# Seven quarter-block products for the gate columns as well, in 14 of 31 pairs, with small changes to the attention values and the first network

## The chip, the core and the metric

The kernel runs on one core of one Trainium2 chip. The metric is the device time of one execution in microseconds (us), as the median of several runs. All numbers below are of that core.

The core's engines work side by side, each through its own list of instructions in order: TensorE (matrix products; PE in the profile, PEld for the loading of its weights), VectorE (DVE), ScalarE (ACT), GpSimd (POOL) and SyncE (SP), which here issues the transfers from memory. Products land in PSUM, where this kernel has eight tiles of 128 x 512 numbers; everything else is in SBUF.

## What is computed

An encoder trunk of two layers on 512 tokens of width 1024, float32. Each layer is a half feed-forward network, a mixer, and another half network; then comes a last norm.

```python
def swiglu(x, w_gate, w_up, w_down):
    return (jax.nn.silu(x @ w_gate) * (x @ w_up)) @ w_down
...
    for i in range(DEPTH):
        x = x + 0.5 * swiglu(rms_norm(x, ffn_norm[i, 0]), ffn_w_gate[i, 0], ffn_w_up[i, 0], ffn_w_down[i, 0])
        hx = rms_norm(x, mix_norm[i])
        j = i // 2
        if i % 2 == 0:
            x = x + mixer_ab(hx, ab_w_in[j], ab_w_out[j], a_q_norm[j], a_k_norm[j], b_rpb[j], cos, sin)
        else:
            x = x + mixer_cd(hx, cd_w_in[j], cd_w_out[j], c_conv_w[j], d_conv_w[j], d_norm_g[j], d_norm_b[j])
        x = x + 0.5 * swiglu(rms_norm(x, ffn_norm[i, 1]), ffn_w_gate[i, 1], ffn_w_up[i, 1], ffn_w_down[i, 1])
    return rms_norm(x, final_norm)
```

The inner width of a network is 2816, that is 22 block columns of 128. mixer_ab is two kinds of attention side by side: "a", 8 heads over all tokens, and "b", 8 heads over a neighbourhood of a grid with a learned bias. mixer_cd is two kinds of convolution.

## The kernel before

**Number format and matmuls.** x lies transposed: 8 slices of 128 channels by 512 tokens. Each float32 operand is split in a rounded high half and the rest, and a product is three matmuls, high by high, high by low, low by high (mm3, lines 126 to 128). A weight piece of 128 x 512 is split when it is needed: ScalarE casts the high half (wh, line 146), VectorE subtracts for the low one (wl, line 147); in mixers GpSimd does some of these. The halves wh and wl have five buffers each.

**Weights.** plan() lists all transfers (units, 512 KB each as a rule) and the pieces that they are cut in, in the order of use. piece() hands out the next one and has the pieces up to three later loaded and split in program order. Plain weight tiles have three buffers (raw), those of the up columns in pairs two more (ux).

**A network.** ffn() goes over the 22 block columns f. A single block is a gate product and an up product of 8 slices each (chunk, 24 matmuls of 512 columns), then gated() and gate(): PSUM times rB (the norm's factor), Silu, in the last network times rB again (fold is False there), times the up product, split. From f = 4 to 19, blocks go by twos through pair(): the gate products stay as they are, but the two up products are one 2 x 2 block product that is done by seven products of quarter blocks in place of eight. For those, halves() makes four combinations of the inputs (tt) once for each network, in four steps, each called by next(prep); pair() needs all four steps. sums() makes four combinations of the weights (lines 92 to 95, VectorE), and seven products of 4 slices (12 matmuls of 256 columns each) are put together by a ScalarE copy (line 358) and seven VectorE additions (line 355). Between the seven products pair() sets two slices of the gate products at a time (blocks). Four networks have eight pairs each. At the end of a network come the down products, 8 x 22 slices of 512 columns.

**First network.** It begins with f = 0 and 1 together, while x still arrives; f = 2 and 3 are single blocks, and after the gate product and the up product of each one step of halves() is set.

**Attention.** mixer_ab() runs 64 units (a head and a quarter of the tokens each; 0 to 31 of kind "a", 32 to 63 of kind "b") in a pipeline written out by hand for TensorE: scores of unit i, transposes of unit i-3 (turn, line 710), weighted values of unit i-5 (mix). Between them fill() takes steps, one slice of a product each, from a list of fillers: values(1) (32 steps), b_project(1) and (2) (32), outs[0] (8), b_project(3) (16), outs[1] (24). How many is set by an account, due, that begins at 2.4 and grows by 1.6 a unit up to unit 31 and by 1.45 after; done counts the steps taken. The last keys, from b_project(3), must be there at unit 51 (five ahead of the first unit that uses them); if they aren't, the while loop runs fillers until they are, and these count as done. put() takes the values out of PSUM: in the second half, f = PSUM times r (by ScalarE or VectorE in turn, lines 595 and 597), then twice a cast by GpSimd (606) and a subtraction by VectorE (607).

**Order.** The program is written with tiles and pools. A planner with a time model of its own sets each engine's order when the kernel is built; in the attention part TensorE's order is the written one. A new tile waits until the one before in its buffer has no reader left. Temporaries t have 10 buffers, PSUM tiles 4 ("g"), 2 ("d") and 2 ("m").

Of the kernel before, what the change touches and what calls it, by code (L numbers as in the profile page):

```python
# [23 lines left out]
PAIRS = (4, 20)  # L24
# [4 lines left out]
class Trunk:  # L29
# [29 lines left out]
    def plan(self, units):  # L59


        self.units, self.pieces = [], []
        for u in units:
            i = len(self.units)
            if len(u) == 4:
                g0, g1, u0, u1 = u
                self.units += [(g0, False), (u0, True), (u1, True), (g1, False)]
                A, B = slice(0, 512), slice(512, 1024)
                self.pieces += [(i, A), (i + 1, A), (i + 1, B), (i, B), (i + 2, 0), (i + 2, 1), (i + 3, A), (i + 2, 2), (i + 2, 3), (i + 3, B), (i + 2, B)]
                continue  # L70
            src, cut = u
            self.units.append((src, False))
# [5 lines left out]
    def load(self, upto):  # L78
        while len(self.loaded) < min(upto + 1, len(self.units)):
            src, held = self.units[len(self.loaded)]  # L80
            t = (self.ux if held else self.raw).tile([P, 1024], F32, tag="raw", name=self.name("raw"))
# [136 lines left out]
    def ffn(self, own, gain, natural=False, start=False):  # L218
# [4 lines left out]
        with self.tc.tile_pool(name=self.name("hp"), bufs=NF) as hp, self.tc.tile_pool(name=self.name("ux"), bufs=2) as self.ux, self.tc.tile_pool(name=self.name("tp"), bufs=4) as tp:  # L223
            hs, held = [], []
            if start:
# [13 lines left out]
                xs = list(self.xs)  # L239
            prep = self.halves(hp, tp, own)  # L240
            f = 2 if start else 0
            while f < NF:
                if PAIRS[0] <= f < PAIRS[1]:
                    self.go(prep)
                    hs += self.pair(hp, xs, fold)
# [14 lines left out]
                else:  # L260
# [5 lines left out]
                    next(prep, 0)  # L266
# [61 lines left out]
    def pair(self, hp, xs, fold):  # L328

# [3 lines left out]
        gates = [self.ps("g"), self.ps("g")]  # L333
        both = ((j, n) for j, ps in enumerate(gates) for n, _ in enumerate(self.chunk(ps, xs)))
        sn, uu, u0 = self.t(), self.t(), self.t()
        gate = []

        def blocks(n):
            for _ in range(n):
                j, k = next(both)  # L340
                if k == NK - 1:
                    gate.append(self.gated(gates[j], fold))

        def product(tag, x):
            ps = self.ps(tag, 256)
# [10 lines left out]
        blocks(2)  # L356
        q1 = product("g", b11)
        nc.scalar.copy(sn[:, L], q1)
        blocks(2)
        add(u0[:, L], product("d", b21), sn[:, L])  # L360
        blocks(2)
        add(sn[:, R], product("d", part(1)), sn[:, L])
        blocks(2)
        q5 = product("g", part(0))
        add(u0[:, R], q5, sn[:, R])
        blocks(2)
        add(uu[:, L], product("d", part(2)), sn[:, R])
        add(uu[:, R], q5, uu[:, L])
        blocks(2)
        add(u0[:, R], product("d", b22), u0[:, R])  # L370
        blocks(2)
        q4 = product("d", part(3))
        h0 = self.t()
        nc.vector.tensor_tensor(h0, u0, gate[0], op=ALU.mult)
        out = [self.hidden(hp, h0)]
        blocks(2)
        add(uu[:, L], q4, uu[:, L])
        h1 = self.t()
        nc.vector.tensor_tensor(h1, uu, gate[1], op=ALU.mult)
        return out + [self.hidden(hp, h1)]  # L380
# [204 lines left out]
    def put(self, t, p, half):  # L585
# [6 lines left out]
        if half == 1:  # L592
            f = self.t()[:, :n]
            if t % 2 == 0:
                nc.scalar.activation(f, p[:, :n], AF.Copy, scale=r)
            else:
                nc.vector.tensor_scalar(f, p[:, :n], r, 1.0, op0=ALU.mult, op1=ALU.mult)
            p, r = f, None
# [5 lines left out]
        for src, hi, lo in parts:  # L604
            if half == 1:
                nc.gpsimd.tensor_copy(hi, src)
                nc.vector.tensor_tensor(lo, src, hi.bitcast(F32), op=ALU.subtract)
                continue
# [186 lines left out]
    def mixer_ab(self, gain):  # L795
        nc = self.nc
        with ExitStack() as ctx:
# [22 lines left out]
            with self.tc.manual_schedule(engines={mybir.EngineType.PE}):  # L820
# [6 lines left out]
                for i in range(n + 5):  # L827
# [7 lines left out]
                    due += (1.6 if i < 32 else 1.45) / 2  # L835
# [3 lines left out]
                    due += (1.6 if i < 32 else 1.45) / 2  # L839
# [253 lines left out]
    def ffn_units(self, i):  # L1093
        a = self.a
        u = []
        for f in range(NF):
# [6 lines left out]
            elif PAIRS[0] <= f < PAIRS[1]:  # L1103
# [119 lines left out]
```

## Time and profile before

| | us |
|---|---|
| median of 3 runs | 1828.51 |
| these runs | 1827.61 to 1831.22 |
| the profiled execution | 1826.34 |
| its span, first to last instruction | 1824.6 |
| TensorE busy in it | 1805.4 |
| VectorE busy | 1240.1 |
| ScalarE busy | 842.7 |

The profile is a trace of every instruction with start, duration, source line and tiles, and a page that sums it up. L126 is line 126 of the kernel. A name such as psg<-xs,wh says what is written and what is read, buffer numbers left out: psg and psd are PSUM tiles of tags "g" and "d", xs the split input, h the split hidden values, tt the input combinations, wh and wl the weight's halves, t a temporary. Ends of matmuls are modelled, and they overlap, so distances between starts tell what one costs. "[1.81 <-ACT wh L146]" after a row means that the engine had been idle for 1.81 us until that instruction was done.

### The profile page before, as it was taken

The numbers are of one execution on the slowest core, as the hardware profiler recorded it, in microseconds if no ns is written. First come the engines' busy times: TensorE is split into PE (matmuls) and PEld (weight loads), VectorE is DVE, ScalarE is ACT, GpSimd is POOL, SyncE is SP. The second block draws the span as 40 slices with busy tenths as digits, with TensorE's granted clock in tenths as the row PEclk, the third lists the DMA queues.
The fourth block names the chain that finished last, engine by engine and source line by source line (L and its number), as shares of the span: only waits on it lengthen the run. The fifth ranks groups of instructions, "written<-read, shape, count | busy, mean of one in ns | idle before, by whom it ended". The sixth has DMA issues, their size and how long they took to land.

```text
span 1824.6 us, 25574 instructions
## 1 busy us (share of the span) xinstructions
PE 1805.4 (99%) x9532; PEld 1555.3 (85%) x9532; DVE 1240.1 (68%) x2211; ACT 842.7 (46%) x1536; POOL 187.2 (10%) x213
## 2 busy tenths in 40 slices
PE   9999999999999999999999999999999999999997
PEld 7899888889878899988888999888888889998886
DVE  6877734488987877764448777634499688887333
ACT  6544433357776544443335444433364554444332
POOL 0000000004432000000000000000389100000000
PEclk9999999999999999999999999999999999999999
DMA  5232233333243232333332332233322232323332
GB/s 198 81 105 93 93 96 95 98 103 99 68 132 114 94 103 96 102 113 96 96 101 81 101 108 93 89 95 96 126 93 93 81 105 94 103 99 96 92 100 66
DMA packets 57675, 181.79 MB, mean 100 GB/s; under 512 B 6352, under 2 KB 8656, under 8 KB 57552
## 3 DMA queue, kind: packets, MB, share of 16 engines
q1 hardware_dynamic: 56976, 179.33, 31.1%
q8 instruction: 75, 1.23, 0.3%
q10 hardware_dynamic: 576, 0.84, 0.1%
q14 instruction: 48, 0.39, 0.1%
HBM read 175.43 MB, written 2.10 MB: 97 GB/s over the span
## 4 chain that ended last, share of the span: by engine, by line
PE 94%; DVE 4%; ACT 1%; DMA 1%; issue 1%; DVEq 0%; SPq 0%; ACTq 0%
PE psg L127 16%; PE psg L126 16%; PE psg L128 16%; PE psd L127 15%; PE psd L128 15%; PE psd L126 15%; PE psm L710 1%; DVE pt L717 1%; DVE wl L147 0%; DMA bias<-in_bias 0%; PE psg L740 0%; PE psg L739 0%; DVE m L673 0%; DVE t L690 0%; PE psg L672 0%
## 5 line engine op out<-in xcount | busy, mean ns | idle before, releaser
L146 ACT CAST wh<-raw 128x512 fp32r<-128x512 f32 (+1 forms) x630 | 380.2, 606 | 616.4 <-PE psd L127 411.9
L147 DVE TENSOR_TENSOR wl<-raw,wh 128x512 fp32r<-128x512 f32 (+1 forms) x556 | 374.5, 674 | 303.3 <-ACT wh L146 297.8
L127 PE MATMUL psg<-xs,wh 128*128 128x512 f32 (+1 forms) x1200 | 455.6, 380 | 0.3 <-DVE xs L156 0.3
L126 PE MATMUL psg<-xs,wh 128*128 128x512 f32 (+1 forms) x1200 | 455.2, 380 | 0.6 <-ACT xs L155 0.6
L128 PE MATMUL psg<-xs,wl 128*128 128x512 f32 (+1 forms) x1200 | 453.2, 378 | 0.0
L128 PE MATMUL psd<-h,wl 128*128 128x512 f32 (+1 forms) x726 | 277.9, 383 | 0.0
L127 PE MATMUL psd<-h,wh 128*128 128x512 f32 (+1 forms) x726 | 277.9, 383 | 0.0
L126 PE MATMUL psd<-h,wh 128*128 128x512 f32 (+1 forms) x726 | 277.7, 383 | 0.0
L128 PEld LDWEIGHTS psg<-xs,wl 128*128 128x128 f32 x1200 | 225.9, 188 | 41.2
L126 PEld LDWEIGHTS psg<-xs,wh 128*128 128x128 f32 x1200 | 226.5, 189 | 37.4 <-ACT xs L155 1.2
L127 PEld LDWEIGHTS psg<-xs,wh 128*128 128x128 f32 x1200 | 226.5, 189 | 36.7 <-DVE xs L156 0.9
L147 POOL TENSOR_TENSOR wl<-raw,wh 128x512 fp32r<-128x512 f32 (+1 forms) x74 | 97.5, 1328 | 766.4 <-ACT wh L146 766.2
L126 PEld LDWEIGHTS psd<-h,wh 128*128 128x128 f32 x726 | 136.4, 188 | 26.8
L128 PEld LDWEIGHTS psd<-h,wl 128*128 128x128 f32 x726 | 136.4, 188 | 26.6
L127 PEld LDWEIGHTS psd<-h,wh 128*128 128x128 f32 x726 | 136.4, 188 | 26.4
L146 ACT CAST wh<-t 128x512 fp32r<-128x512 f32 x128 | 79.4, 621 | 88.2 <-PE psg L127 47.7
L355 DVE TENSOR_TENSOR t<-psd,t 128x256 f32<-128x256 f32 x160 | 67.8, 423 | 71.2 <-PE psd L128 71.2
L126 PE MATMUL psd<-tt,wh 128*128 128x256 f32 x384 | 108.5, 283 | 1.8 <-ACT wh L146 1.8
L128 PE MATMUL psd<-tt,wl 128*128 128x256 f32 x384 | 108.9, 284 | 0.1
L127 PE MATMUL psd<-tt,wh 128*128 128x256 f32 x384 | 108.7, 283 | 0.0
L126 PE MATMUL psd<-xs,wh 128*128 128x256 f32 (+1 forms) x344 | 108.1, 314 | 0.0
L128 PE MATMUL psd<-xs,wl 128*128 128x256 f32 (+1 forms) x344 | 106.9, 311 | 0.0
(275 smaller groups left out, 2702.6 us busy)
## 6 DMA issues: line engine op xcount, KB each, us to landing
raw<-in_up SPq DMA_DIRECT2D x83, 512.0 KB, 3.6
raw<-in_gate SPq DMA_DIRECT2D x83, 512.0 KB, 3.5
raw<-in_down SPq DMA_DIRECT2D x64, 448.0 KB, 3.3
raw<-in_down SPq DMA_DIRECT2D x32, 512.0 KB, 3.5
raw<-in_cdin SPq DMA_DIRECT2D x18, 512.0 KB, 3.5
raw<-in_abqk SPq DMA_DIRECT2D x13, 512.0 KB, 3.5
raw<-in_about SPq DMA_DIRECT2D x16, 256.0 KB, 2.7
bias<-in_bias SPq DMA_DIRECT2D x8, 512.0 KB, 3.5
```

What stands on the lines that cost most here:

```text
L126: mm(ps, lhsT=aH, rhs=bH, start=first, stop=False)
L127: mm(ps, lhsT=aH, rhs=bL, start=False, stop=False)
L128: mm(ps, lhsT=aL, rhs=bH, start=False, stop=last)
L146: self.nc.scalar.copy(hi, src)
L147: (eng or self.nc.vector).tensor_tensor(lo, src, hi.bitcast(F32), op=ALU.subtract)
L355: add = lambda to, a, b: nc.vector.tensor_tensor(to, a, b, op=ALU.add)
L710: nc.tensor.transpose(ps[:, i * P : (i + 1) * P], pr[:, i * P : (i + 1) * P], self.ident)
L717: nc.vector.tensor_tensor(lo, src, hi.bitcast(F32), op=ALU.subtract)
```

## The change

In 14 pairs, listed in BOTH (three in the first network, four in the second and third, three in the last), the two gate products are done by seven quarter-block products as well, with the four sums of the gate weights and the seven additions that belong to them; the gate's seven come before the up's seven, with no other product between. The old body of pair() becomes seven(), a generator that yields the two results. Results are multiplied in place. The 17 other pairs keep their order of products; the first join is now written after the last product. The first network has its first pair at f = 6 in place of 4, so it has seven pairs, and calls one step of halves() for each of f = 2 to 5 instead of two. put() of the second half no longer goes over a temporary: ScalarE makes the high half from PSUM, VectorE the low half from PSUM. due grows by 1.6 up to unit 31, by 1.8 from 32 to 50 and by 1.35 after.

```diff
-PAIRS = (4, 20)
+PAIRS = ((6, 20), (4, 20), (4, 20), (4, 20))
+BOTH = ((8, 12, 16), (6, 10, 14, 18), (6, 10, 14, 18), (6, 12, 18))
...
+            if len(u) == 5:
+                g0, g1, u0, u1, both = u
+                if both:
+                    self.units += [(g0, 1), (g1, 2), (u0, 3), (u1, 3)]
+                    for j in (i, i + 2):
+                        self.pieces += [(j, slice(0, 512)), (j, slice(512, 1024))]
+                        self.pieces += [(j + 1, n) for n in range(4)] + [(j + 1, slice(512, 1024))]
+                    continue
...
-            t = (self.ux if held else self.raw).tile([P, 1024], F32, tag="raw", name=self.name("raw"))
+            t = (self.ux if held == 3 else self.raw).tile([P, 1024], F32, tag="raw", name=self.name("raw"))
...
-                    next(prep, 0)
+                    if not start:
+                        next(prep, 0)
...
+    def seven(self, xs, tags, between):
...
+        def product(x):
+            between()
+            ps = self.ps(next(tags), 256)
...
+        nc.scalar.copy(sn[:, L], product(b11))
+        add(u0[:, L], product(b21), sn[:, L])
+        add(sn[:, R], product(part(1)), sn[:, L])
+        q5 = product(part(0))
+        add(u0[:, R], q5, sn[:, R])
+        add(u1[:, L], product(part(2)), sn[:, R])
+        add(u1[:, R], q5, u1[:, L])
+        add(u0[:, R], product(b22), u0[:, R])
+        yield u0
+        add(u1[:, L], product(part(3)), u1[:, L])
+        yield u1
+
+    def pair(self, hp, xs, fold, both):
+
+        nc = self.nc
+        gate, out = [], []
+        if both:
+            for g in self.seven(xs, "gdggdgd", lambda: None):
+                nc.vector.tensor_tensor(g, g, self.rB, op=ALU.mult)
+                nc.scalar.activation(g, g, AF.Silu)
+                if not fold:
+                    nc.vector.tensor_tensor(g, g, self.rB, op=ALU.mult)
+                gate.append(g)
+            between = lambda: None
+        else:
+            gates = [self.ps("g"), self.ps("g")]
+            blocks = ((j, n) for j, ps in enumerate(gates) for n, _ in enumerate(self.chunk(ps, xs)))
+
+            def between():
+                for _ in range(2):
+                    j, k = next(blocks)
+                    if k == NK - 1:
+                        gate.append(self.gated(gates[j], fold))
+
+        def join(u):
+            nc.vector.tensor_tensor(u, u, gate[len(out)], op=ALU.mult)
+            out.append(self.hidden(hp, u))
+
+        ups = self.seven(xs, "gdggdgd" if both else "gddgddd", between)
+        first = next(ups)
+        if both:
+            join(first)
+            join(next(ups))
+        else:
+            last = next(ups)
+            join(first)
+            between()
+            join(last)
+        return out
...
-        if half == 1:
-            f = self.t()[:, :n]
-            if t % 2 == 0:
-                nc.scalar.activation(f, p[:, :n], AF.Copy, scale=r)
-            else:
-                nc.vector.tensor_scalar(f, p[:, :n], r, 1.0, op0=ALU.mult, op1=ALU.mult)
-            p, r = f, None
...
         for src, hi, lo in parts:
-            if half == 1:
-                nc.gpsimd.tensor_copy(hi, src)
-                nc.vector.tensor_tensor(lo, src, hi.bitcast(F32), op=ALU.subtract)
-                continue
             nc.scalar.activation(hi, src, AF.Copy, scale=r)
             nc.vector.scalar_tensor_tensor(lo, src, r, hi.bitcast(F32), op0=ALU.mult, op1=ALU.subtract)
...
-                    due += (1.6 if i < 32 else 1.45) / 2
+
+                    due += (1.6 if i < 32 else 1.8 if i < 51 else 1.35) / 2
```

## Rows read from the trace of the kernel before

**Rows 1.** The page: span, first line of part 1, shares of the chain in part 4
```profile
span 1824.6 us, 25574 instructions
PE 1805.4 (99%) x9532; PEld 1555.3 (85%) x9532; DVE 1240.1 (68%) x2211; ACT 842.7 (46%) x1536; POOL 187.2 (10%) x213
...
PE 94%; DVE 4%; ACT 1%; DMA 1%; issue 1%; DVEq 0%; SPq 0%; ACTq 0%
```

**Rows 2.** Timeline of TensorE in one pair: start us, duration us, engine, line, tiles
```profile
100.35 0.40 PE L126 MATMUL psg<-xs,wh 128*128 128x512 f32 x1
...
101.73 0.28 PE L126 MATMUL psd<-xs,wh 128*128 128x256 f32 x1
...
103.17 0.40 PE L126 MATMUL psg<-xs,wh 128*128 128x512 f32 x1
```

**Rows 3.** Chain that ended last, in order of time: start us, length us, what
```profile
109.30 0.35 PE psg L128 x2
130.38 0.35 PE psg L128 x2
```

**Rows 4.** Windows: stretch, length, busy us (count) of PE, PEld, DVE, ACT, POOL; clock, DMA
```profile
130.38:151.46 21.08, 21.08 (x134) 19.06 (x134) 16.34 (x29) 9.40 (x16) 0.00 (x0) 1.00 0.30 101
1534.37:1555.43 21.06, 21.06 (x135) 19.04 (x134) 17.44 (x31) 9.31 (x16) 0.00 (x0) 1.00 0.29 100
```

**Rows 5.** Timeline of TensorE near the end, two matmuls of one run
```profile
1803.04 0.28 PE L127 MATMUL psd<-h,wh 128*128 128x256 f32 x1
...
1807.24 0.28 PE L126 MATMUL psd<-h,wh 128*128 128x256 f32 x1
```

**Rows 6.** Timeline of VectorE where it works without a break
```profile
143.85 0.68 DVE L147 TENSOR_TENSOR h<-t,h 128x512 fp32r<-128x512 f32 x1
144.45 0.68 DVE L95 TENSOR_TENSOR t<-raw,t 128x512 f32<-128x512 f32 x1
...
146.26 0.42 DVE L355 TENSOR_TENSOR t<-psd,t 128x256 f32<-128x256 f32 x1
146.59 0.68 DVE L147 TENSOR_TENSOR wl<-raw,wh 128x512 fp32r<-128x512 f32 x1
```

**Rows 7.** Waits from 109 to 152 us: us in total, times, longest
```profile
ACT wh L146 <- PE psd L127: 8.2, 8, 1.7
```

**Rows 8.** First network: windows as above, then the timeline of TensorE
```profile
40.00:58.00 18.00, 18.00 (x93) 15.34 (x92) 18.00 (x40) 13.12 (x29) 0.00 (x0) 1.00 0.16 56
58.00:64.00 6.00, 3.77 (x14) 2.11 (x13) 6.00 (x14) 3.68 (x8) 0.00 (x0) 0.89 0.04 3
...
58.89 0.39 PE L128 MATMUL psg<-xs,wl 128*128 128x512 f32 x1
61.09 0.39 PE L126 MATMUL psd<-tt,wh 128*128 128x256 f32 x1 [1.81 <-ACT wh L146]
...
65.61 0.41 PE L128 MATMUL psd<-tt,wl 128*128 128x256 f32 x1
65.83 0.40 PE L126 MATMUL psd<-tt,wh 128*128 128x256 f32 x1
```

**Rows 9.** Attention: VectorE's scores, a window as above, a wait of TensorE (timelines)
```profile
533.05 0.41 DVE L690 CUSTOM_DVE_ANT_0 t<-psg,bias 128x256 f32<-128x256 f32 x1
...
540.18 0.42 DVE L690 CUSTOM_DVE_ANT_0 t<-psg,bias 128x256 f32<-128x256 f32 x1 [0.22 <-PE psg L688]
...
540.00:548.00 8.00, 5.06 (x40) 4.52 (x39) 6.97 (x26) 7.15 (x20) 2.75 (x5) 1.00 0.77 214
...
469.12 0.63 PE L710 MATMUL psm<-ident,t 128*128 128x128 f32 x4 [0.92 <-DVE pt L717]
```

**Rows 10.** Lines 597, 606 and 610: duration ns min/median/max, first and last start
```profile
L597 DVE TENSOR_SCALAR t<-psd,rc x2: 603/604/606, 441.4 to 464.8; 128x384 f32<-128x384 f32 x2
...
L606 POOL CAST v<-t x8: 343/347/473, 441.1 to 467.9; 128x192 fp32r<-128x192 f32 x8
...
L610 DVE SCALAR_TENSOR_TENSOR v<-psg,rc,v x12: 275/284/343, 413.3 to 418.6; 128x64 fp32r<-128x64 f32 x8, 128x128 fp32r<-128x128 f32 x4
```

More of the change, by code (lines that the diff above doesn't have):

```diff
@@ L64, in plan @@
             i = len(self.units)
-            if len(u) == 4:
-                g0, g1, u0, u1 = u
-                self.units += [(g0, False), (u0, True), (u1, True), (g1, False)]
+            if len(u) == 5:
[6 more added lines that the diff above has]
+                    continue
+                self.units += [(g0, 0), (u0, 3), (u1, 3), (g1, 0)]
                 A, B = slice(0, 512), slice(512, 1024)
@@ L71, in plan @@
             src, cut = u
-            self.units.append((src, False))
+            self.units.append((src, 0))
             w = src.shape[1]
@@ L239, in ffn @@
                 xs = list(self.xs)
+            p0, p1 = PAIRS[own // 8]
             prep = self.halves(hp, tp, own)
@@ L242, in ffn @@
             while f < NF:
-                if PAIRS[0] <= f < PAIRS[1]:
+                if p0 <= f < p1:
                     self.go(prep)
-                    hs += self.pair(hp, xs, fold)
+                    hs += self.pair(hp, xs, fold, f in BOTH[own // 8])
                     f += 2
@@ L326, in halves @@
             yield
-    def pair(self, hp, xs, fold):
+    def seven(self, xs, tags, between):
         nc = self.nc
         L, R = slice(0, 256), slice(256, 512)
[L333 to L345, printed above, removed]
+        sn, u0, u1 = self.t(), self.t(), self.t()
+        tags = iter(tags)
+        def product(x):
+            between()
+            ps = self.ps(next(tags), 256)
             h, l = self.piece()
@@ L355, in pair @@
         add = lambda to, a, b: nc.vector.tensor_tensor(to, a, b, op=ALU.add)
[L356 to L364, printed above, removed]
-        add(u0[:, R], q5, sn[:, R])
-        blocks(2)
-        add(uu[:, L], product("d", part(2)), sn[:, R])
-        add(uu[:, R], q5, uu[:, L])
@@ L369, in pair @@
[L369 to L380, printed above, removed]
+        nc.scalar.copy(sn[:, L], product(b11))
+        add(u0[:, L], product(b21), sn[:, L])
@@ L838, in mixer_ab @@
                         pts[i - 3] = self.turn(units[i - 3], prs.pop(i - 3))
-                    due += (1.6 if i < 32 else 1.45) / 2
+                    due += (1.6 if i < 32 else 1.8 if i < 51 else 1.35) / 2
                     done += self.fill(int(due) - done)
@@ L1102, in ffn_units @@
                 u += [(w[:, c : c + 512], 512) for c in (0, 512) for w in (g, v)]
-            elif PAIRS[0] <= f < PAIRS[1]:
+            elif PAIRS[i][0] <= f < PAIRS[i][1]:
                 if f % 2 == 0:
-                    u.append((g, a["gate"][i, f + 1], v, a["up"][i, f + 1]))
+                    u.append((g, a["gate"][i, f + 1], v, a["up"][i, f + 1], f in BOTH[i]))
             else:
```

## The prediction

> **What bounds the kernel now.** I read the page first. TensorE is busy 99% of the span and carries 94% of the chain that ended last [rows 1], so a change pays by what it takes off TensorE, or off the few places where TensorE stands still. Busy time there is modelled and overlaps, so the price of a matmul is the distance between starts in the timeline. Six matmuls of 512 columns start from 100.35 to 101.73 us, 0.23 us each; twelve of 256 columns from there to 103.17 us, 0.120 us each [rows 2]. Half the columns cost 52% of the time. In the chain the same point of the loop over pairs returns after 21.08 us [rows 3]. A pair has 2 gate blocks x 8 slices x 3 matmuls = 48 of 512 columns and 7 up products x 4 slices x 3 = 84 of 256. 84 x 0.120 = 10.08 us; the other 11.00 us are the gate, 0.229 us a matmul. TensorE is never idle in this stretch. VectorE is the next engine: 16.34 of 21.08 us, and 17.44 in the last network, which multiplies each gate by rB a second time (fold is false) [rows 4].
>
> **The gate by seven products (14 pairs).** Removed: 48 x 0.229 = 11.00 us. Added: 84 x 0.120 = 10.08 us. TensorE's share of such a pair becomes 168 x 0.120 = 20.16 us, 0.92 us less; 14 x 0.92 = 12.9 us, all of it on the bounding engine. The pace in a long unbroken run of 256 columns is read at the tail of the kernel: 35 matmuls from 1803.04 to 1807.24 us are again 0.120 us apart [rows 5], although every one brings its own weights.
>
> What this costs lies on VectorE. Instructions of 512 columns in a pair before: 11 splits (L147), 4 sums (L92 to L95), 2 times rB (L285), 2 joins (L374, L379), 2 splits of the result: 21; and 7 additions of 256 (L355). After: 14 splits, 8 sums, 2, 2, 2 = 28, and 14 additions. One takes 0.68 or 0.42 us, but in an unbroken stretch the next starts after 0.60 and 0.33 us [rows 6]. So VectorE goes from 21 x 0.60 + 7 x 0.33 = 14.9 us to 28 x 0.60 + 14 x 0.33 = 21.4 us, against 20.16 us on TensorE: over by 1.2 us. In the last network two more make it 22.6 us, over by 2.5. This is covered in two ways. First, between two such pairs there is at least one of the old kind with some 6 us free (5 in the last network); two together are 36.3 of 41.2 us, and in the last network one and two old ones 54.8 of 62.3. Second, the halves wh and wl have five buffers, and ScalarE's cast waits for TensorE to free one [rows 7], so it works ahead as far as buffers allow: four products of 1.44 us are 5.8 us, less a cast and a split, about 4.1 us of cover by estimate. 2.5 is under 4.1. The gate's four sums, moreover, are issued three pieces early, during the pair before. I charge 0.1 us a pair, 1.4 us; the ends are 0 and 0.92 us (the whole gain). I take a value near the low end, since the pair of now, without a stall at 78% of VectorE, is nearer to 88% than the saturated stretch below is.
>
> The Trainium skill speaks against this ("VectorE: DVE Perf Modes", section "The DRAIN you can't avoid"): the next VectorE instruction is said not to start until the pipeline of the one before has emptied. By that a pair would need 28 x 0.68 + 14 x 0.42 us, 24.9. The starts 0.60 us apart beside durations of 0.68 [rows 6] disagree; the rule is kept as the first rival all the same.
>
> Smaller things in these pairs. ScalarE gets three more casts and one copy for 20 us, and has 9.4 of 21 us in use [rows 4]. The loads are the same four of 512 KB on SP's queue, but both gate columns now go before both up columns: an up load queued behind the second gate load waits if no raw buffer is free. They have three, and the DMA engines are busy 0.30 [rows 4]. The third and fourth gate sums may need the temporary that the previous pair's u0 and u1 held, so they wait for its joins (four or five steps of about 0.6 us); they are needed 5.8 and 7.2 us into the pair. All these I cost at nothing; without cover each shows as a wait of TensorE for a cast. In old-kind pairs joining in place removes two temporaries and no instruction: nothing.
>
> **First network, start.** Now the pair at f = 4 needs all four steps of halves() at once. VectorE is busy 18.00 of 18 us from 40 to 58 us, and then TensorE waits for a cast: the matmuls from 58.89 to 65.83 us, 3 of 512 and 14 of 256 columns (three of the run's rows stand here), are worth 0.69 + 1.68 = 2.4 us and take 6.94 [rows 8]. 4.6 us are lost, part of it idle, the rest at a granted clock of 0.89 on average over 58 to 64 us, with starts 0.21 us apart where 0.12 is the pace [rows 8]; that is the lower level, 1.2 GHz, after the idle time. The change makes f = 4 and 5 single blocks and runs one step of halves() in each of f = 2 to 5 instead of two in f = 2 and 3. That costs 96 x 0.229 - 21.08 = 0.9 us. A step is five operations and three splits of 256 columns, about 3 us; a single block has 4 splits, rB, product and result, 7 x 0.60 = 4.2 us, so 7.2 of 11 us: VectorE no longer piles up. Forecast -4.6 + 0.9 = -3.7 us, ends +0.9 (the stall merely moves to f = 6) and -3.7.
>
> **Attention.** Units 0 to 63 each get filler steps by an account (due). The 48 + 40 = 88 steps before outs[1] (values, three projections, first two output rows) must be through before unit 51 needs the last keys; by the old account 2.4 + 32 x 1.6 + 19 x 1.45 = 81 are. The missing seven are run at a stroke: no score is taken between 533.05 and 540.18 us [rows 9]. Then the account is ahead, no filler comes for some five units, and TensorE has nothing but the chain of softmax: 5.06 of 8 us busy from 540 to 548 us [rows 9]. With 1.8 the account is 2.4 + 51.2 + 34.2 = 87.8 when unit 51 comes. The burst goes, and so do 2.9 us. The rest, 18 x 1.35 = 24.3, is what the 24 steps of outs[1] want.
>
> The values of the second half lose a scaling copy into a temporary (0.60 us on VectorE in two of four tiles, one on ScalarE in the others) and GpSimd's casts, 0.35 us, eight of them; ScalarE and VectorE read PSUM instead. The new pairs of instructions aren't in the trace at 192 columns; those at 64 and 128 take 0.28 us on VectorE [rows 10]. Removed on VectorE 2 x 0.60; added, by estimate, at most 8 x 0.15 for reading PSUM; about even. ScalarE gains eight casts of some 0.4 us and loses two copies of some 0.6, an estimate from the VectorE rows: 2 us in 40. The PSUM tile is freed later, after both pairs instead of one copy. Against it stands the way over GpSimd, where the normalization of the weights queues; TensorE waits 0.92 us in this stretch [rows 9]. I take -0.5, ends -1.3 and +2. Attention together -3.4 us.
>
> **Sum.** -12.9 + 1.4 - 3.7 - 3.4 = -18.6 us. The profiled execution took 1826.34 us (span 1824.6 and 1.7 around it), 2.2 below the median of 1828.51; 1807.7 for it, and 1809.9 against the median.
>
> **Rivals.**
> 1. VectorE becomes the bound. If instructions cost their whole duration, a new pair lasts 24.9 us on VectorE (26.3 in the last network), less 20.16 and the cover of 4.1: 0.6 and 2.0 us of stall. 11 x 0.6 + 3 x 2.0 = 12.6 us eat the pairs' gain; with -3.7 and -3.4 the time is 1821. A half of it is as likely as the whole. Against: rows 6. Chance 0.10.
> 2. Slower: VectorE's lateness in a new pair passes the 4.1 us of cover, TensorE stands still, and its clock falls as at 58 us. One such event costs 4.6 us [rows 8]; in all 14 pairs 64 us, and 1873. The kernel is slower from the fifth such pair on ((12.9 + 3.7 + 3.4) / 4.6 = 4.3). For: VectorE is saturated inside the pair, and its order is fixed when the kernel is built. Against: 1.2 to 2.5 us of excess. Chance 0.05.
> 3. Attention gives nothing or loses (+2): the stall at 540 us was not the account's doing, or ScalarE is now late. -11.5 - 3.7 + 2 = -13.2, 1815. Chance 0.15.
> 4. The change doesn't take what it says off TensorE: in runs of 168 the weight loads set the pace at more than 0.120 us. At 0.126 the gain of a pair is gone, 1822. Against: rows 5. Chance 0.02.
>
> **How the numbers follow.** The forecast, 1809.9 us, has 0.68 and its own range 1806 to 1814 (everything in full and the charge of 1.4 gone, 1807, with a little for the scatter of runs; or the first network's half and 0.3 us a pair). The range of 8 in 10 takes in rival 3 and half of rival 1: 1805.5 to 1818. Faster by over 0.2% (3.7 us, about what a measurement of this kernel can tell from none): 0.88; within 0.2%: 0.06, from the worse half of rival 1; slower: 0.06.
>
> **What would show it.** Right: new pairs of 20.2 us in the chain and old ones of 21.1, TensorE without waits in either; no low clock from 58 to 66 us; TensorE busy throughout 540 to 548 us; VectorE near full in the new pairs and slack behind them. Wrong: TensorE waiting for wh or wl in a new pair, first of all in the last network; additions (L355) before which TensorE waits for a PSUM buffer; a stall at f = 6; longer waits of L710 from 430 to 475 us.

## The result and the profile after

| | before | after |
|---|---|---|
| median, us | 1828.06 | 1808.81 |
| runs, us | 1827.51 to 1831.22 | 1807.73, 1808.46, 1809.15 |
| ratio to before | | 0.9889 [0.987, 0.9909] |
| the profiled execution, us | 1826.34 | 1809.15 |
| its span | 1824.6 | 1807.4 |

The changed kernel is faster by 1.1%; the forecast was 1809.9 us. A fourth execution of the changed kernel took 3197.5 us at a mean granted clock of 0.722; the median of 1808.81 counts it (the three listed have 1808.46), the ratio leaves it out. The two profiled executions lie 17.2 us apart and the medians 19.3: the profiled execution of before was 1.7 us under its median, that of after is the longest of the three listed. What follows is told of the traces, so it accounts for 17.2 us.

In the new listing mm3 is lines 134 to 136, ScalarE's cast line 154, VectorE's split 155, the joins 393, the scores 686 and 702, the transposes 725, put() around 625, and the statistics of the "a" queries and keys (a_scales, one step of the program before the attention units) 567.

First the page (span; busy time, share and instructions of each engine; the chain by engine), to be held against [rows 1]:

```profile
span 1807.4 us, 26840 instructions
PE 1793.5 (99%) x10000; PEld 1570.1 (87%) x10000; DVE 1297.8 (72%) x2391; ACT 868.0 (48%) x1594; POOL 183.2 (10%) x205
...
PE 98%; DVE 1%; DMA 1%; issue 0%; ACT 0%; SPq 0%; DVEq 0%
```

The waits of TensorE from 50 to 1700 us (us in total, times, longest):

```profile
PE psg L702 <- DMA bk<-bk: 1.1, 1, 1.1
PE psd L134 <- DVE v L625: 0.9, 2, 0.6
PE psm L494 <- DVE rp L155: 0.3, 1, 0.3
PE psm L725 <- DVE rz L713: 0.2, 1, 0.2
```

TensorE is still the bound, with 11.9 us less of busy time. VectorE has 57.7 us more. All the waits listed belong to the attention part; between 50 us and the tail TensorE waits for nothing in any pair.

The chain at one point of the loop (start us, length us, what), answering [rows 3]:

```profile
125.97 0.35 PE psg L136 x2
...
167.23 0.35 PE psg L136 x2
...
208.49 0.35 PE psg L136 x2
```

Windows (length; busy us and count of PE, PEld, DVE, ACT, POOL; clock; DMA), answering [rows 4, 8, 9]:

```profile
58.00:64.00 6.00, 6.00 (x28) 4.95 (x27) 2.88 (x7) 2.78 (x6) 0.00 (x0) 1.00 0.40 138
135.30:155.46 20.16, 20.16 (x169) 20.10 (x168) 19.24 (x38) 11.34 (x20) 0.00 (x0) 1.00 0.30 97
400.00:405.00 5.00, 5.00 (x24) 5.00 (x25) 3.44 (x15) 2.63 (x5) 0.00 (x0) 0.50 0.00 0
540.00:548.00 8.00, 6.91 (x42) 5.77 (x40) 6.65 (x22) 5.64 (x17) 2.39 (x5) 1.00 0.54 164
1570.57:1590.73 20.16, 20.16 (x168) 20.07 (x167) 19.71 (x39) 11.27 (x20) 0.00 (x0) 1.00 0.33 97
```

A new and an old pair together take 41.26 us, twice in a row. A new pair is 20.16 us of TensorE without a gap, in the first network (135.30) and in the last (1570.57), while VectorE is at 95% and 98%. Its matmuls start 0.120 us apart in unbroken runs of 158 (148 in the last network); the planner sets the last few among the products of the pair behind. The stall at 58 us is gone: 6.00 busy of 6.00 at full clock. From 540 to 548 us TensorE is busy 6.91 us where it was 5.06. And a granted clock of 0.50 stands over all of 400 to 405 us, outside the pairs.

Where the 17.2 us come from, by the first matmul of each part (the down products mark the end of a network's pairs):

| part | before, us | after, us | difference |
|---|---|---|---|
| to the first down product of network 1 | 245.79 | 239.59 | -6.20 |
| from there to the first matmul of network 2 (attention) | 348.64 | 347.91 | -0.73 |
| network 2 to its first down product | 234.39 | 230.79 | -3.60 |
| down products of network 2, network 3 to its first down product | 354.07 | 350.47 | -3.60 |
| from there to the first down product of the last network | 508.70 | 506.04 | -2.66 |
| the rest | 132.96 | 132.56 | -0.40 |

Networks 2 and 3 have four new pairs each: 0.90 us a pair. The last has three: 0.89. Three in the first network would be 2.7, which leaves 3.5 us of its 6.20 to the new start; this is a remainder, and the unchanged first network alone differs by up to 0.6 us between traces (245.79 before, 246.42 in e3).

### The profile page after: what moved, and what is told of

Same layout as the page of the kernel before. It is cut to its first block, busy times and chain, and to the rows that moved or that the text cites. A ratio compares the mean times of both kernels' runs of the same rounds, so it can differ in the third digit from the quotient of the medians.

```text
span 1807.4 us, 26840 instructions
## 1 busy us (share of the span) xinstructions
PE 1793.5 (99%) x10000; PEld 1570.1 (87%) x10000; DVE 1297.8 (72%) x2391; ACT 868.0 (48%) x1594; POOL 183.2 (10%) x205
## 4 chain that ended last, share of the span: by engine, by line
PE 98%; DVE 1%; DMA 1%; issue 0%; ACT 0%; SPq 0%; DVEq 0%
PE psg L134 16%; PE psg L135 16%; PE psd L135 16%; PE psd L134 16%; PE psg L136 16%; PE psd L136 16%; PE psm L725 1%; PE psg L755 1%; PE psg L754 1%; DMA bk<-bk 0%; PE psg L687 0%; PE psg L686 0%; DMA x<-in_x 0%; PE psm L567 0%; PE psg L702 0%; PE psg L703 0%
## 5 line engine op out<-in xcount | busy, mean ns | idle before, releaser
L154 ACT CAST wh<-raw 128x512 fp32r<-128x512 f32 (+1 forms) x617 | 372.1, 606 | 582.0 <-PE psd L135 333.0
L155 DVE TENSOR_TENSOR wl<-raw,wh 128x512 fp32r<-128x512 f32 (+1 forms) x543 | 364.3, 672 | 295.9 <-ACT wh L154 288.7
L135 PE MATMUL psg<-xs,wh 128*128 128x512 f32 (+1 forms) x1156 | 419.9, 364 | 0.0
L134 PE MATMUL psg<-xs,wh 128*128 128x512 f32 (+1 forms) x1156 | 419.5, 364 | 0.3 <-ACT xs L163 0.2
L136 PE MATMUL psg<-xs,wl 128*128 128x512 f32 (+1 forms) x1156 | 418.0, 363 | 0.0
L136 PEld LDWEIGHTS psg<-xs,wl 128*128 128x128 f32 x1156 | 218.2, 189 | 33.4
L134 PEld LDWEIGHTS psg<-xs,wh 128*128 128x128 f32 x1156 | 218.7, 189 | 32.0 <-ACT xs L163 1.4
L135 PEld LDWEIGHTS psg<-xs,wh 128*128 128x128 f32 x1156 | 218.6, 189 | 31.0 <-DVE xs L164 0.8
L154 ACT CAST wh<-t 128x512 fp32r<-128x512 f32 x180 | 108.9, 621 | 146.2 <-DVE t L101 52.0
L155 DVE TENSOR_TENSOR wl<-t,wh 128x512 fp32r<-128x512 f32 x180 | 120.9, 685 | 0.3 <-ACT wh L154 0.2
L135 PE MATMUL psd<-tt,wh 128*128 128x256 f32 x428 | 121.0, 283 | 0.0
L136 PE MATMUL psd<-tt,wl 128*128 128x256 f32 x428 | 120.9, 282 | 0.0
L134 PE MATMUL psd<-tt,wh 128*128 128x256 f32 x428 | 120.6, 282 | 0.0
```

Of the source, the lines that this page charges most:

```text
L134: mm(ps, lhsT=aH, rhs=bH, start=first, stop=False)
L135: mm(ps, lhsT=aH, rhs=bL, start=False, stop=False)
L136: mm(ps, lhsT=aL, rhs=bH, start=False, stop=last)
L154: self.nc.scalar.copy(hi, src)
L155: (eng or self.nc.vector).tensor_tensor(lo, src, hi.bitcast(F32), op=ALU.subtract)
```

## The experiments

### The parts, each alone

Four kernels hold one part of the change each, over the new program text. e1 has the 14 pairs; e2 the first network's start; e3 the account; e4 put().

- e1 keeps the new BOTH. PAIRS begins at 4 in each network, next(prep, 0) is called always, and due and put() are those of before.
- e2 keeps the new PAIRS and the new calls of next(prep, 0). BOTH is empty; due and put() are those of before.
- e3 keeps the new due. BOTH is empty; PAIRS, the calls of next(prep, 0) and put() are those of before.
- e4 keeps the new put(). BOTH is empty; PAIRS, the calls of next(prep, 0) and due are those of before.

The line by which three of them empty BOTH:

```diff
-BOTH = ((8, 12, 16), (6, 10, 14, 18), (6, 10, 14, 18), (6, 12, 18))
+BOTH = ((), (), (), ())
```

> The rewritten pair() with the 14 new pairs, and nothing else of the change: the first network starts its pairs at f = 4 as before, the values go over the temporary, and the account of fillers is the old one. Theory: TensorE bounds the pairs and VectorE stays covered, so each new pair lasts 20.16 to 20.2 us and the kernel gains 14 x 0.9 = 12.6 us, about 1815.5. The stall at 58 us and the starved stretch at 540 us stay. Rival, that part of the 17 us comes from the smaller edits and the new pairs stall here or there: a gain of 9 us or less, with waits of TensorE for wh or wl in new pairs.

> The rewritten pair() without any new pair, values and account as before; only the first network has its first pair at f = 6 and one step of halves() in each of f = 2 to 5. Theory: the stall of 4.6 us at 58 us with its low clock is gone and one pair becomes two single blocks for 0.9 us: -3.7 us, about 1824.4. Rival: the stall moves to f = 6, and the change costs up to 0.9 us.

> The rewritten pair() without any new pair, first network and values as before; only the account of fillers grows by 1.8 from unit 32 to 50 and by 1.35 after. Theory: no seven fillers at a stroke at unit 51 and no starved stretch behind, -2 to -3 us. The trace of the changed kernel shows the stretch from the scores of unit 51 to the end of attention shorter by 2.2 us. Rival, that the stretch was not the account's doing and TensorE waits elsewhere for the same time: within 0.5 us of before.

> The rewritten pair() without any new pair, first network and account as before; only the values of the second half go straight from PSUM. Theory: about even, -0.5 us, between -1.3 and +1; the scores of units 10 to 32 keep their distances. Rival: the two more operations on ScalarE for each tile, or the PSUM tile that is freed later, hold up TensorE between 425 and 470 us: +1 to +2 us, and this is where the attention's missing gain went. A second rival for the missing gain: the low clock around the small products of a_scales, which lasted 3.4 us in the kernel before and 6.8 us in the changed one; it should then vary from kernel to kernel whatever the edit, by about 1.6 us.

| | median, us | ratio [95%] | us of 1828 |
|---|---|---|---|
| e1, pairs | 1817.71 | 0.9936 [0.9922, 0.995] | -11.7 |
| e2, start | 1828.74 | 0.9996 [0.9987, 1.0005] | -0.7 |
| e3, account | 1825.64 | 0.9983 [0.9974, 0.9992] | -3.1 |
| e4, values | 1828.14 | 0.9992 [0.9983, 1.0001] | -1.5, not told from none |
| sum | | | -17.0 |
| all four | 1808.81 | 0.9889 [0.987, 0.9909] | -20.3 |

The pairs give nearly what they were expected to (the second network takes 230.79 us in e1, as in the changed kernel, and 234.39 in e2, e3 and e4, as before: the rewritten text alone moves nothing there), the account too. The start alone gives nothing in the median, although its network ends at 242.14 us in the trace, 3.65 earlier than before, as forecast. In the traced execution a part of the gain is taken back in the attention part, which is 2.1 us longer than before. A window there, in e2:

```profile
540.00:548.00 8.00, 6.05 (x24) 5.27 (x25) 5.25 (x19) 4.42 (x15) 2.80 (x6) 0.57 0.44 113
```

Two rows of TensorE's timeline about it (there are more), with the waits that they begin with:

```profile
539.05 0.52 PE L736 MATMUL psm<-ident,pb 128*128 128x128 f32 x3 [1.54 <-DVE pt L743]
...
543.42 0.55 PE L713 MATMUL psg<-bk,bq 128*128 128x256 f32 x1 [1.11 <-DMA bk<-bk]
```

This is the starved stretch behind the burst that the old account makes [rows 9]: TensorE waits 1.54 and 1.11 us, and the clock goes to the lower level, 0.57 on average over these 8 us, where the window of before has 1.00. e1 and e4, which have the old account too, show the same stretch at 0.79 and 0.96; the window cuts their low clock off, which begins later (at 544.67 and 547.38 us) and lasts 6.8 us in e1, as in e2, and 3.4 us in e4. e3, with the new account, shows 1.00 and 7.21 of 8 us busy. So with the old account one and the same stretch is dear in some executions and cheap in others, and e2's ten runs scatter from 1825.2 to 1831.1. The traced one is the shortest of the ten, and the other nine have no trace: that the low clock there is what keeps the gain out of the median is likely, not shown.

### The start undone in the changed kernel

```diff
-PAIRS = ((6, 20), (4, 20), (4, 20), (4, 20))
+PAIRS = ((4, 20), (4, 20), (4, 20), (4, 20))
...
-                    if not start:
-                        next(prep, 0)
+                    next(prep, 0)
```

> The changed kernel with the first network's edit undone: pairs from f = 4, two steps of halves() in each of f = 2 and 3. Done alone that edit gained only 0.4 us in the median (-2.4 to +0.9), though its trace shows the first network's up and gate part 3.7 us shorter; the kernels with the old account have a starved stretch at 540 us in which the clock falls in some executions. Theory: the edit is worth its 3.7 us, and what hid them was that low clock, which the new account takes away; undone here it costs +3.7 us against the changed kernel, about 1812.5, -0.86% against before. Rival: the edit is worth nothing, since what it saves comes back in attention: about 1809, -1.05%.

Measured: 1811.67 us, 0.9909 [0.9894, 0.9923], 0.20% or 3.7 us more than with it; the two intervals overlap. The trace is plainer. The stall is back, as this window shows:

```profile
58.00:64.00 6.00, 3.56 (x15) 2.05 (x13) 6.00 (x15) 3.94 (x9) 0.00 (x0) 0.98 0.00 0
```

3.56 busy of 6 us, where [rows 8] has 3.77, and the first down product comes at 243.90 us, 4.3 later than in the changed kernel. The attention part is 2.0 us shorter in this execution; 1.6 of it lie ahead of the scores, where the low clock at a_scales lasts 3.4 us and not 6.8 (below). By the traces the start is worth 3.5 to 4.3 us in its network, alone (3.65) and in the whole (4.3); neither median shows it clear of the error.

### All 31 pairs new

```diff
-BOTH = ((8, 12, 16), (6, 10, 14, 18), (6, 10, 14, 18), (6, 12, 18))
+BOTH = (range(6, 20, 2), range(4, 20, 2), range(4, 20, 2), range(4, 20, 2))
```

> The changed kernel with all 31 pairs of the new kind. By TensorE alone this would be 17 x 0.92 = 15.6 us less, 1793. Theory: without an old pair between, VectorE sets the pace, 21.4 us a pair where rB is multiplied once and 22.6 in the last network, less the cover of about 4 us once a network: 7 x 21.4 + 16 x 21.4 + 8 x 22.6 = 673 us less 16 of cover, 657, against 14 x 20.16 + 17 x 21.08 = 641 in the changed kernel: +16 us, about 1825, with waits of TensorE for wh and wl and a VectorE without gaps. If the waits bring the clock down, as at 58 us in the kernel before, each event costs up to 4.6 us more and it is slower than before. Rival, that VectorE is no bound at this work (its starts come closer still, or joins and sums overlap otherwise): below 1800.

Measured: 1839.65 us, 1.006 [1.0045, 1.0075]. It is slower than before, and by more than was expected. Windows in which new pairs follow each other, in the second and the last network:

```profile
637.35:807.68 170.33, 166.88 (x1345) 162.58 (x1343) 169.01 (x330) 84.88 (x160) 0.00 (x0) 1.00 0.31 97
1503.45:1679.20 175.75, 168.64 (x1314) 159.84 (x1313) 175.17 (x340) 82.80 (x158) 0.00 (x0) 1.00 0.29 91
```

The first two rows of the waits of TensorE over its whole span:

```profile
PE psd L134 <- ACT wh L154: 9.7, 34, 0.3
PE psg L136 <- DVE wl L155: 7.1, 36, 0.2
```

VectorE is busy 99% and 99.7%: here it is the bound. The first joins of two pairs in a row, in VectorE's timeline of the second and of the last network:

```profile
701.61 0.68 DVE L393 TENSOR_TENSOR t<-t,t 128x512 f32<-128x512 f32 x1
...
723.11 0.68 DVE L393 TENSOR_TENSOR t<-t,t 128x512 f32<-128x512 f32 x1
...
1571.93 0.68 DVE L393 TENSOR_TENSOR t<-t,t 128x512 f32<-128x512 f32 x1
...
1594.63 0.68 DVE L393 TENSOR_TENSOR t<-t,t 128x512 f32<-128x512 f32 x1
```

So a pair takes 21.50 us, and 22.70 in the last network, where the starts of [rows 6] had given 21.4 and 22.6 and TensorE needs 20.16. By the Trainium skill's sentence in "The DRAIN you can't avoid" (page "VectorE: DVE Perf Modes") that the next instruction does not start until the pipe is empty it would have been 24.9 by estimate, as the prediction worked out from durations; the measured pace decides against that here. The same paragraph lets an instruction that is not held start earlier.

Why it is dearer than expected: 1.34 us of excess in each of eight pairs is 10.7 us; eight times 0.90 is 7.2 us of gain, so a network without cover would be 3.5 us longer than before. The second is 1.8 longer (236.2 against 234.4), so its cover, over eight pairs together, is 1.7 us; the third, by the part of the table above, is 1.3 longer (355.4 against 354.1), which makes 2.2. In the last, at 2.54 us of excess a pair, the same sum gives 13.2 without cover, and 11.0 were measured (519.7 against 508.7): 2.2 again. The first, with seven pairs, would be 3.1 longer than in e2, which has none there, and is 3.2 longer (245.33 against 242.14): no cover. The prediction had put it at about 4.1.

The waits are many and short: 70, none over 0.3 us, and the clock is 1.00 in both windows. So lateness in waits this short did not bring the clock falls of rival 2.

### How large the cover is

c2 has 18 new pairs; in each of the first three networks there are two places where two follow each other.

```diff
+BOTH = ((8, 10, 14, 16), (6, 8, 12, 14, 18), (6, 8, 12, 14, 18), (6, 10, 14, 18))
```

> The changed kernel with 18 new pairs instead of 14: two in a row at most (f = 8, 10, 14, 16 in the first network; 6, 8, 12, 14, 18 in the second and third; 6, 10, 14, 18 in the last). Theory: with all pairs new, VectorE set a pace of 21.5 us a pair (22.7 in the last network) and fell behind TensorE only after about 2 us of cover in each network. Two in a row are 2 x 1.3 = 2.7 us over; an old pair behind gives 6 us back. So four more pairs give 4 x 0.9 = 3.6 us, less a stall of 0 to 0.7 us in each of six places: 1805 to 1809 against 1808.8. Rival, that a new pair needs an old one on both sides: a stall of 1.3 us or more at each of the six places, 1813 or more.

Measured: 1807.83 us, 0.9884 [0.9868, 0.9901], from the changed kernel's 0.9889 not to be told. Networks 2 and 3 have one more new pair (two places with two in a row) and are 0.5 us longer each: the second takes 231.27 us against 230.79, the third, with the down products ahead of it, 350.93 against 350.47. The waits of TensorE in the second network:

```profile
PE psg L136 <- DVE wl L155: 0.4, 2, 0.2
```

Two short waits for two such places. They make 0.4 us together, while the network lost 1.4 (the 0.90 that the added pair should have gained and the 0.48): ends of matmuls are modelled, so a wait can begin under the end that is drawn, and the list then shows it too short. That is 0.7 us a place; two pairs in a row are 2 x 1.34 = 2.7 us over, so about 2.0 us are covered. That agrees with e5: the cover is some 2 us, half of the estimate.

The last network, whose four new pairs in c2 still stand apart, gains 1.0 us by the added one (505.05 against 506.04, by the part of the table). Over all four networks the four more pairs give nothing: -0.1, +0.5, +0.5 and -1.0 us by the traces.

e6 takes the suspected cover away: three buffers for wh and wl in place of five.

```diff
-        self.wh = pool("wh", 5)
-        self.wl = pool("wl", 5)
+        self.wh = pool("wh", 3)
+        self.wl = pool("wl", 3)
```

> The changed kernel with three buffers for wh and for wl in place of five. Theory: VectorE's excess of 1.3 us in a new pair (2.5 in the last network) is covered because it works ahead as far as these buffers allow, and two fewer take 2 x 1.44 = 2.9 us of that away: stalls of 0.2 to 1.4 us in each of 11 new pairs and 1.5 to 2.9 in the last three, in sum +7 to +24 us, nearly all of it in the new pairs and little in the old ones. Rival, that the cover is the old pairs' free time and the sums that are issued early, and not these buffers: less than +3 us.

Measured, one execution: 1852.06 us. Networks 2 and 3 are 5.89 us longer each (the second takes 236.68), or 1.5 us for each new pair. Windows over an old and a new pair of the second:

```profile
660.00:681.00 21.00, 21.00 (x153) 19.94 (x152) 17.36 (x33) 10.33 (x18) 0.00 (x0) 1.00 0.27 87
681.00:702.00 21.00, 19.95 (x147) 18.79 (x146) 19.83 (x38) 10.24 (x19) 0.00 (x0) 1.00 0.31 85
```

All waits of TensorE in that network:

```profile
PE psd L134 <- ACT wh L154: 2.6, 4, 0.6
PE psg L134 <- ACT wh L154: 1.6, 4, 0.4
```

The old pair runs full (21.00 of 21), the new one loses 1.05 us in its window; 1.5 us a pair is about the 1.34 us of excess, with nothing left to cover it. This speaks for the buffers as the cover in these networks. It does not settle it: in the last network, where 2.54 us are over and two old pairs lie between, the same edit costs 0.84 us a pair (229.97 against 227.45 us from its first matmul to its first down product), so about 1.7 us are covered there even with three buffers. What covers them no run shows. (In the attention part the same edit costs 13 us and in the second mixer 4.6, so the total says nothing of the pairs.)

e7 was to add VectorE work to each new pair, seven additions into a tile that the pair doesn't read, so as to find where the cover ends.

```diff
+        if both:
+            more = iter(range(7))
+
+            def between():
+                if next(more, None) is not None:
+                    nc.vector.tensor_tensor(self.S, self.x[0], self.x[1], op=ALU.add)
```

> The changed kernel with seven more VectorE additions of 512 columns (into a tile that nobody reads) in the second half of each new pair, 4.2 us. Theory: a new pair needs 25.7 us on VectorE (26.9 in the last network), 5.5 (6.7) over TensorE's 20.16; cover of 2 to 4.4 us leaves 1.1 to 3.5 us of stall (2.3 to 4.7), +19 to +53 us in all, as many short waits of TensorE for wh and wl. Rival 2 of the prediction: the waits join to one in which the clock falls; then some 4.6 us a pair on top, and a granted clock below 1 in the new pairs.

Measured, one execution: 1829.36 us. It doesn't answer the question, for the additions did not land where they were written: they depend on nothing in the pair, and the planner set them earlier. Of the second network's 28, 16 run from 590 to 640 us, 12 from 640 to 680, none after. It shows something else. Once in each network a wait comes that the lower level of the clock follows: of 3.11 us in the first, ahead of its pairs, and of 1.64, 1.15 and 2.38 us in the others. A window of the second:

```profile
660.00:680.00 20.00, 17.85 (x130) 17.04 (x130) 19.79 (x38) 9.75 (x19) 0.00 (x0) 0.91 0.26 83
```

The wait in it, from TensorE's timeline:

```profile
673.25 0.38 PE L134 MATMUL psg<-tt,wh 128*128 128x256 f32 x1 [1.64 <-ACT wh L154]
```

The idle time is 2.15 us in this window, the clock 0.91 on average; the four networks lose 4.8, 7.1, 4.1 and 5.5 us against the changed kernel, 5.4 on average, against the 4.6 that rival 2 put down for such an event. The second network has a further wait of 1.15 us (at 614.49 us), after which the clock did not fall. The price was about right, and in the changed kernel its condition did not arise.

### The low clock at 400 us

TensorE's timeline at a_scales in the changed kernel (start us, length us, line, tiles, form, count):

```profile
396.70 4.46 PE L567 MATMUL psm<-sel,sq 128*128 128x2 f32 x32
401.02 0.56 PE L134 MATMUL psg<-wh,xs 128*128 128x256 f32 x1
...
402.87 0.41 PE L136 MATMUL psg<-wh,xs 128*128 128x256 f32 x1
403.08 0.41 PE L134 MATMUL psg<-wh,xs 128*128 128x256 f32 x1
```

Thirty-two products of two columns each, with no idle time ahead of any row, and behind them 256-column matmuls that start 0.21 us apart in place of 0.12. The clock is 0.50 from 399.29 us, in the midst of these products, to 406.12, 6.8 us. Before, the same step is followed by 3.4 us at 0.50, as this window shows:

```profile
407.40:410.81 3.41, 3.41 (x18) 3.41 (x17) 2.27 (x12) 2.27 (x4) 0.00 (x0) 0.50 0.00 0
```

What it costs can be read from all fourteen traces, for the way from the first down product of network 1 to the first scores takes one of three times: 177.4 us in the four traces without a low clock there (e2, c2, e8, c3), 178.9 to 179.1 in the seven with 3.4 us of it, 180.5 in the three with 6.8. So it costs 1.5 and 3.1 us. The difference, 1.6 us, is most of what the attention part is short of its forecast. e8 divides the step in four groups of eight, with products of full slices between them:

```diff
+            if t:
+                yield
...
-            (4, 48): [lambda: self.a_scales([q[1] for q in qs])],
+            (4, 33): [lambda: scales.append(self.a_scales([q[1] for q in qs])), lambda: next(scales[0])],
+            (4, 42): [lambda: next(scales[0])],
+            (4, 51): [lambda: next(scales[0])],
+            (4, 60): [lambda: next(scales[0], 0)],
```

> The changed kernel with the 32 small products of a_scales (two columns each, 112 ns apart, 3.5 us in a row) set in four groups of eight with nine matmuls of 256 columns between. In the trace of the changed kernel the clock is low for 6.8 us from the middle of the row on, in the kernel before for 3.4 us. Theory: with full matmuls between, the clock doesn't fall there, and the 1.7 to 3.4 us that it cost are gone: -1.5 to -3.4 us against the changed kernel, 1805.5 to 1807.3. Rival: the clock falls for another reason, or later scales hold up the first scores: 1809 or more.

Measured: 1807.37 us (1805.29 to 1808.65), 0.9884 [0.9869, 0.9899]; just above what was expected and 0.05% below the changed kernel, which is within the error; its shortest run lies 2.4 us below the other's shortest. Windows of its trace:

```profile
394.00:399.00 5.00, 5.00 (x47) 5.00 (x45) 4.87 (x8) 1.76 (x4) 0.00 (x0) 1.00 0.64 184
399.00:404.00 5.00, 5.00 (x43) 4.91 (x43) 4.03 (x13) 2.85 (x5) 0.00 (x0) 1.00 0.00 0
```

Two of the four groups in TensorE's timeline:

```profile
394.80 0.95 PE L569 MATMUL psm<-sel,sq 128*128 128x2 f32 x8
...
396.77 0.95 PE L569 MATMUL psm<-sel,sq 128*128 128x2 f32 x8
```

The same 32 matmuls, the clock at 1.00 throughout. Of the twelve traces with the step undivided, ten have the low clock at it or just behind, 3.4 us in before, e1, e3, e4, e7, e9 and u1, 6.8 in the changed kernel, e5 and e6; e2 and c2 have none. Of the two with it divided (e8, c3) none has. So the row of tiny matmuls is the likely cause, on few traces; against the execution of the changed kernel that was traced, dividing saves 3.1 us; that it is worth 2 us in the median is not shown, and what makes the low stretch 3.4, 6.8 or nothing with the same step stays open.

### The last keys' transfer

At 1.1 us the longest wait after is for the keys' DMA (bk) at the first scores that use the last projection. e9 lets the account reach that projection sooner.

```diff
-                    due += (1.6 if i < 32 else 1.8 if i < 51 else 1.35) / 2
+                    due += (1.6 if i < 32 else 1.95 if i < 51 else 1.2) / 2
```

> The changed kernel with an account that grows by 1.95 from unit 32 to 50 and by 1.2 after: the last keys are projected two units earlier. In the changed kernel TensorE still waits 1.1 us at 543 us for the copy of these keys by the DMA queue. Theory: the wait goes, -1.2 us, 1807.6. Rival: the slower fill after unit 51 leaves TensorE short again, +0.5 to +2 us.

Measured: 1810.78 us, 0.9906 [0.989, 0.9923], if anything 2 to 3 us more. The waits of TensorE from 490 to 590 us:

```profile
PE psm L725 <- DVE pt L732: 1.7, 2, 1.4
PE psm L725 <- POOL pb L715: 0.8, 1, 0.8
PE psm L725 <- DVE rz L713: 0.8, 1, 0.8
```

The wait for the DMA is gone from the list, and 3.3 us of waits for the softmax stand in its place, which fits the rival: fillers spent early are missing behind.

### Together

c3 is c2's pairs and e8's spreading.

> The same 18 pairs, and the small products of a_scales in four groups with full matmuls between. Theory: both gains add up, 1.4 us below the kernel with 18 pairs alone; the clock stays at its higher level through a_scales. Rival: the clock's fall moves elsewhere in attention, and nothing is left of the 1.4 us in the median.

Measured: 1805.95 us (1805.51 to 1806.57), 0.9871 [0.9856, 0.9886]. It is the lowest of all by its median, 0.18% under the changed kernel; the intervals overlap, so it is not shown to be faster. The traces give the added pairs no part in it: of c3 and e8, neither of which has the low clock, c3 has the longer span, 1804.3 us against 1803.5.

## Why the prediction came out right

The time was right (1809.9 against 1808.81), and the working is right in its two larger terms and wrong in the third; that the total came so close is in part luck, as the sum below shows.

- **Pairs.** Forecast 12.9 less a charge of 1.4. The traces show 0.90 us a pair, 12.6 in all. The pace of 0.120 us held over runs of 158 matmuls (rival 4 falls), and of the charge 0.3 was needed. VectorE's 21.4 and 22.6 us, from the distance between starts, were right to 0.1 (e5), and so rival 1 falls.
- **The cover.** Right that there is one; that it is the buffers' is borne out in networks 2 and 3 by e6 and not in the last. Wrong in its size, 2 us and not 4.1 (by the durations of a cast, 0.61 us, and a split, 0.68, the prediction's own sum gives 4.5). This did not matter, as the excess of a single new pair is 1.34 us with an old pair behind it; in the last network the excess of 2.54 is above it, and TensorE still shows no wait there (1570.57) and gains 0.89 us a pair, which no run explains. The 14 pairs lie close to the limit: 18 gain no more that can be told, 31 lose 31 us against the 14.
- **First network.** Forecast -3.7; measured -3.5 as the remainder, -3.65 alone (e2) and -4.3 in the whole (u1). No stall appeared at f = 6. VectorE's 7.2 of 11 us a block was a sound reading: it is busy 7.86 us from 58 to 69 us and 7.54 from 69 to 80.
- **Attention.** Forecast -3.4, measured -0.73 in the trace. Rival 3 was near it in size; of its reasons the first did not hold, since the stretch at 540 us was the account's doing (e3), and the second holds for 0.9 us. The starts of the scores divide it: first "a" at 424.7 us before and 420.1 after, first "b" at 497.7 and 493.3, last "b" at 559.3 and 556.4. From the first "b" to the last it is 1.5 longer, from there to network 2 4.0 shorter: the account's part is -2.5, where -2.9 was said. The burst and the starved stretch went, a DMA wait of 1.1 us is left. From the first "a" to the first "b", where put() works, it is +0.2, where -0.5 was said. The wait of 0.92 us at the transposes [rows 9] is gone, L725 waits 0.2 us in all; but TensorE now waits 0.9 us for put() (L625 in the list of waits above), so the PSUM tiles are freed later, as was feared. One of the new subtractions from PSUM takes 0.40 us on VectorE, where from the temporary it took 0.34; so it is 0.06 us more, and not the 0.15 that was allowed. From the first down product to the first "a" it is +1.6. The step that failed is one that the prediction did not have: it took the part ahead of the scores as unmoved, and there the low clock at a_scales grew from 3.4 to 6.8 us, which makes the 1.6.
- **The sum.** Against the profiled execution -18.6 was said and -17.2 came: the pairs gave 1.1 more than was said, the attention 2.7 less. The medians lie 19.3 apart, since the traced execution of before was 1.7 under its median and that of after 0.3 above; so forecast and median meet by errors of both signs and by which executions were traced.
- **Rival 2.** Price about right (5.4 against 4.6), condition absent: lateness on VectorE shows first as waits of 0.2 to 0.3 us, which left the clock at 1.00 (e5).

## What to carry to other kernels

When work moves to a second engine that is nearly full, take its price from the distance between starts in its busiest stretch, not from durations, and place the heavy loops so that a lighter one follows each; the lead between the engines covers the excess of one and most of that of two, not of a row. The gain of a part tried alone can be lost in a part behind it whose time varies, so test it also by taking it out of the whole. Where a stretch is slow in some executions and not in others, compare the traces part by part before the medians.

## What was not expected of the hardware

- At a row of 32 matmuls of two columns without idle time the granted clock fell to 0.50, for 3.4 us (a cost of 1.5 us) or 6.8 us (3.1), in ten of twelve traces; it began within 1.6 us of the row's last start, before or after it. In groups of 8 between 256-column matmuls it fell in none of two.
- Seventy waits of TensorE of at most 0.3 us, over networks in which VectorE is the bound, left the granted clock at 1.00 (e5); single waits of 1.64 to 3.11 us were each followed by the lower level (e7), as was the 1.81 us of [rows 8]. Of shorter ones some were and some were not: 1.15 us in the third network of e7 and 1.30 us at 541.90 us in e1 were, 1.15 us in the second network of e7 and 1.49 us at 546.69 us before were not.
